# A fourth modulation vector of layer 1 computed on VectorE, and its pieces spread over the first FFN

## The chip, the cores and the metric

The kernel runs on one core of a Trainium2 chip. The metric is the device time of one execution in microseconds (us); three timed runs of the kernel before gave 1013.0 to 1016.56, with a median of 1015.02. The trace comes from one further execution of 1012.26 us. Its span, from the first to the last instruction in the trace, is 1010.5 us; the 1.8 us between them lie around the program.

The engines are named as in the trace: PE is TensorE's matmul, DVE is VectorE, ACT is ScalarE, POOL is GpSimd, SP is SyncE, whose queue issues nearly all weight transfers.

## What is computed

A two-layer trunk works on 384 tokens of width 1024: 256 latent tokens, which use the condition vector `c`, and 128 context tokens, which use `c_ctx`. Layer 0 is latent attention, layer 1 differential attention; each is followed by a convolutional FFN. Every sub-layer is modulated by vectors that come from the two condition vectors through one large matrix per layer (adaLN):

```python
cond_ctx = jax.nn.silu(c_ctx)[None, :]
cond_lat = jax.nn.silu(c)
for i in range(DEPTH):
    mod_p = jnp.split((cond_ctx @ ada_w[i] + ada_b[i])[:, None, :], N_MOD, axis=-1)   # N_MOD = 6
    mod_s = jnp.split((cond_lat @ ada_w[i] + ada_b[i])[:, None, :], N_MOD, axis=-1)
    hp = _modulate(yp, norm1_g[i], mod_p[0], mod_p[1])      # _rms(x, g) * (1 + scale) + shift
    ...                                                     # mixer; yp = yp + mod_p[2] * mp
    yp = yp + mod_p[5] * _conv_ffn(_modulate(yp, norm2_g[i], mod_p[3], mod_p[4]), *fprm)
    ...                                                     # the same for ys with mod_s

def _conv_ffn(h, w_in, conv_w, conv_b, w_out):
    a = _dwconv3(h @ w_in, conv_w) + conv_b
    g, up = jnp.split(a, 2, axis=-1)
    return (jax.nn.silu(g) * up) @ w_out
```

So each of the six vectors of a layer is a product of two condition vectors with a 1024x1024 block of `ada_w`. The change is about vector 4 of layer 1, the scale of that layer's FFN. It is first used in the norm ahead of that FFN, behind the whole attention of layer 1.

## The kernel before

**Weights.** Weights come from HBM in pieces of at most 128x1024 fp32 (512 KB) into a ring of seven buffers (`raw`, RAW_BUFS = 7), in the order of the plan below, by one queue on SP. A piece waits in that queue until the piece seven places earlier has been read for the last time. Weights of the big products are split into two fp32r parts, `whi` (a cast on ACT, L237) and `wlo` (a subtraction on DVE, L238), in rings of five pieces each (SPLIT_BUFS = 5), and each product is three matmuls (L320 to L322). Pieces marked WHOLE are read as they are.

**The first FFN.** Its hidden part has 22 steps `ffn0.in`; each takes two weight pieces (halves of the contraction) and gives two 128x384 results in PSUM, `fg` and `fu`, by 48 matmuls (L320 to L322). Behind it come the convolution (ACT L612, then eight DVE operations L614 and L616), SiLU, the product `hx` and its split `xh`, `xl`. Then eight steps `ffn0.out` follow, in the order 1, 2, 5, 3, 6, 0, 4, 7, each with three pieces of `w_out` (1024, 896 and 896 columns), 66 matmuls into `fo`, and the addition to `yT` (DVE L535). After the last, the norm of layer 1 leads to `diff.begin` and its projections `dkq0` (result `pd`).

**Modulation vectors.** They are made in two ways. `ada_block` runs on PE: eight weight pieces (rows of the contraction) are each multiplied by both conditions in four small matmuls on 32 columns of the array (L400); they gather in the PSUM tile `ada` (tag "a", one buffer), which DVE copies out (L414), and two transposes (`adat`, L421) bring it into place. `gemv_block` runs on DVE: eight rows of the transposed matrix are each multiplied by the condition, broadcast over all partitions in `condb`, and summed along the row by the same operation (L442). Each row takes two such operations, one for each condition: the first writes its products into `junk`, the second into the row's own buffer, which it frees. Such an operation is called a column here. Vectors 0, 1 and 3 of layer 1 (`vec0`, `vec1`, `vec3`) are made so, vector 4 (`vec4`) by `ada_block`; the gate of the attention (`gate1a`) also goes through `ada_block` and takes the PSUM tile `ada` behind `vec4`.

**Order.** The string SCHEDULE lists all steps; instructions and weight pieces are emitted in its order, and when the program is built a scheduler with its own estimates may still move instructions within an engine. The order of each engine is then fixed; an instruction that waits holds all behind it on that engine.

Of the kernel before, what the change touches and what calls it, by code (L numbers as in the profile page):

```python
# [186 lines left out]
vec3.5 ffn0.out2 vec3.1 vec3.4 ffn0.out5 ffn0.out3 ffn0.out6 ffn0.out0 vec4.5 vec4.4 gate1a.0 vec4.1 vec3.7 vec3.3
vec3.t vec4.6 vec4.7 ffn0.out4 ffn0.out7 vec4.t gate1a.2 diff.begin dkq0.claim gate1a.3 gate1a.6 dkq0 gate1a.5
gate1a.1 gate1a.4 gate1a.7 dv0.00 gate1a.t dv0.01 dv0.10 dv0.11 dk0.t0 dq0.t1 dv0.20 dq0.t0 diff0.s0 dk1.00 dv0.21
dk1.01 diff0.s1 dk0.t1 dk1.10 dk1.11 dk1.20 dq1.00 dq1.01 diff0.s2 dk1.21 diff1.s0 dq1.10 dq1.11 dq1.20 diff0.t0  # L190
diff1.s1 dq1.21 dk1.t0 dk1.t1 diff0.t2 dv1.00 dv1.01 dk2.00 dk2.01 dv1.10 diff0.t1 dv1.20 dv1.21 dq1.t0 dv1.11
diff1.s2 dq1.t1 diff2.s0 diff0.v dk2.10 diff1.t0 diff1.t2 diff1.t1 dk2.11 dk2.20 diff2.s1 diff2.s2 dk2.21 dq2.00
dq2.01 dq2.10 dq2.11 dk2.t0 diff1.v diff2.t1 dq2.20 diff0.ot dv2.00 diff2.t0 diff3.s0 dq2.t0 diff2.t2 dq2.21 dk2.t1
diff3.s1 diff3.s2 dv2.01 dq2.t1 dv2.10 dv2.11 dv2.20 diff2.v diff4.s0 dk3.00 diff3.t1 dk3.01 diff3.t0 dv2.21 diff1.ot
diff3.t2 diff4.s1 diff4.s2 dk3.10 dk3.20 dk3.21 dk3.11 dq3.00 diff3.v diff2.ot dq3.01 dk3.t0 diff5.s0 dq3.10 dv3.00
dq3.11 diff5.s1 diff4.t1 dk3.t1 dq3.20 diff4.t2 dq3.21 dv3.01 dv3.10 diff5.s2 diff3.ot dq3.t0 diff4.t0 dv3.11 dq3.t1
dv3.20 dv3.21 diff6.s0 wo1.low0 diff4.v diff5.t1 diff6.s1 diff5.t0 diff6.s2 diff5.t2 diff7.s0 diff6.t1 diff5.v
diff4.ot diff7.s1 wo1.low1 diff6.t0 wo1.low4 diff7.s2 wo1.low2 diff6.t2 wo1.low3 diff5.ot wo1.low5 wo1.low6 wo1.part0
diff7.t0 diff6.v diff7.t2 diff7.t1 wo1.low7 diff6.ot diff7.v wo1.part1 diff7.ot diff.end wo1.full2 wo1.full0 wo1.full1
wo1.full3 wo1.full6 ffn1.begin wo1.full4 wo1.full5 wo1.full7 ffn1.norm ffn1.claim gate1f.0 gate1f.1 gate1f.2 gate1f.3  # L200
gate1f.4 gate1f.6 gate1f.5 gate1f.7 gate1f.t ffn1.in01 ffn1.in2 ffn1.in3 ffn1.in4 ffn1.in5 ffn1.in6 ffn1.in7 ffn1.in8
# [1261 lines left out]
```

## Time and profile before

| what | value |
|---|---|
| median of three timed runs | 1015.02 us (1013.0 to 1016.56) |
| profiled execution, its span | 1012.26 us, 1010.5 us |
| PE busy | 984.3 us, 97% of the span |
| DVE busy | 740.4 us, 73% |
| ACT busy | 522.0 us, 52% |
| transfers | 160.54 MB, mean 159 GB/s |
| granted TensorE clock | 0.999 of full speed |

The shares are means over stages that differ much, so each stage is read by itself. The first FFN lies between about 237 and 525 us of the span: its hidden steps to 427 us, its output steps from 428 to 525 us.

### The profile page before, as it was taken

What the parts mean: (1) busy time and instruction counts of PE and PEld (TensorE: products, weight loads), DVE (VectorE), ACT (ScalarE), POOL (GpSimd) and SP (SyncE); (2) the same over time, 40 slices, a digit from 0 to 9 for tenths busy, and PEclk for the clock granted to TensorE, in tenths of its full rate; (3) what the DMA queues carried; (4) which work ended last, traced back from release to release, by engine and by line L of the source; (5) the groups of instructions that cost most, each with busy time, mean ns of one, the idle gap of its engine ahead of it and who ended that gap; (6) DMA issues with size and microseconds to landing.
All of it is one profiled execution on the core that took longest, in us unless ns stands there. A gap on an engine that the chain in (4) does not pass through costs nothing.

```text
span 1010.5 us, 16897 instructions
## 1 busy us (share of the span) xinstructions
PE 984.3 (97%) x6280; PEld 919.0 (91%) x6280; DVE 740.4 (73%) x1860; ACT 522.0 (52%) x1104; POOL 20.6 (2%) x48
## 2 busy tenths in 40 slices
...
GB/s 345 277 281 220 172 93 96 204 68 305 113 171 190 188 180 197 211 234 142 195 213 246 103 100 95 100 90 63 174 203 126 125 126 126 120 115 139 136 57 19
DMA packets 46226, 160.54 MB, mean 159 GB/s; under 512 B 5472, under 2 KB 6752, under 8 KB 46016
## 3 DMA queue, kind: packets, MB, share of 16 engines
...
q8 instruction: 49, 0.80, 0.3%
...
## 4 chain that ended last, share of the span: by engine, by line
PE 87%; DVE 5%; DMA 4%; ACT 2%; issue 1%; POOL 0%; DVEq 0%; ACTq 0%
PE fg L322 6%; PE fg L321 6%; PE fg L320 6%; PE fu L322 6%; PE fu L320 6%; PE fu L321 6%; PE fo L321 5%; PE fo L320 5%; PE fo L322 5%; PE pd L320 3%; PE pd L321 3%; PE pd L322 3%; PE wo L320 2%; PE wo L322 2%; PE wo L321 2%; PE ada L400 2%
## 5 line engine op out<-in xcount | busy, mean ns | idle before, releaser
L237 ACT CAST whi<-raw 128x512 fp32r<-128x512 f32 (+3 forms) x273 | 213.2, 801 | 221.9 <-PE fo L321 91.8
L238 DVE TENSOR_TENSOR wlo<-raw,whi 128x512 fp32r<-128x512 f32 (+3 forms) x273 | 245.0, 909 | 84.9 <-ACT whi L237 77.5
L322 PE MATMUL fg<-hh,wlo 128*128 128x384 f32 x352 | 117.9, 335 | 3.7 <-DVE wlo L238 3.7
L320 PE MATMUL fg<-hh,whi 128*128 128x384 f32 x352 | 118.2, 336 | 0.7 <-ACT hh L527 0.7
L321 PE MATMUL fg<-hl,whi 128*128 128x384 f32 x352 | 118.1, 335 | 0.0
L320 PE MATMUL fo<-xh,whi 128*128 128x384 f32 x352 | 117.8, 335 | 0.0
L320 PE MATMUL fu<-hh,whi 128*128 128x384 f32 x352 | 117.8, 335 | 0.0
L321 PE MATMUL fo<-xl,whi 128*128 128x384 f32 x352 | 117.7, 334 | 0.0
L322 PE MATMUL fu<-hh,wlo 128*128 128x384 f32 x352 | 117.6, 334 | 0.0
L321 PE MATMUL fu<-hl,whi 128*128 128x384 f32 x352 | 117.6, 334 | 0.0
L322 PE MATMUL fo<-xh,wlo 128*128 128x384 f32 x352 | 117.6, 334 | 0.0
L320 PE MATMUL pd<-whi,hh 128*128 128x256 f32 x288 | 83.9, 293 | 0.0
L321 PE MATMUL pd<-wlo,hh 128*128 128x256 f32 x288 | 82.3, 287 | 0.0
L322 PE MATMUL pd<-whi,hl 128*128 128x256 f32 x288 | 81.1, 284 | 0.0
L322 PEld LDWEIGHTS fg<-hh,wlo 128*128 128x128 f32 x352 | 66.1, 188 | 4.4 <-DVE wlo L238 4.3
L320 PEld LDWEIGHTS fg<-hh,whi 128*128 128x128 f32 x352 | 66.1, 188 | 2.0 <-ACT hh L527 1.5
L612 ACT ACTIVATE cva<-fg,small 128x384 f32<-128x384 f32 x44 | 29.7, 675 | 73.8 <-PE fg L322 73.8
L321 PEld LDWEIGHTS fg<-hl,whi 128*128 128x128 f32 x352 | 66.1, 188 | 1.2 <-DVE hl L528 0.8
L320 PEld LDWEIGHTS fo<-xh,whi 128*128 128x128 f32 x352 | 66.1, 188 | 0.8 <-ACT cva L612 0.4
L321 PEld LDWEIGHTS fo<-xl,whi 128*128 128x128 f32 x352 | 66.1, 188 | 0.4 <-issue 0.4
L320 PEld LDWEIGHTS fu<-hh,whi 128*128 128x128 f32 x352 | 66.1, 188 | 0.3
L322 PEld LDWEIGHTS fu<-hh,wlo 128*128 128x128 f32 x352 | 66.1, 188 | 0.0
(323 smaller groups left out, 2075.2 us busy)
## 6 DMA issues: line engine op xcount, KB each, us to landing
...
raw<-in_w_out SPq DMA_DIRECT2D x32, 448.0 KB, 3.4
...
```

The costliest lines, as they stand in the source:

```text
L237: self.nc.scalar.copy(hi[:, c], t[:, c])
L238: self.nc.vector.tensor_tensor(lo[:, c], t[:, c], hi[:, c].bitcast(F32), op=ALU.subtract)
L320: T.matmul(out, wh, xh, start=first, stop=False)
L321: T.matmul(out, wh, xl, start=False, stop=False)
L322: last_mm[0] = T.matmul(out, wl, xh, start=False, stop=last)
L400: T.matmul(st["acc"][32 * j:32 * j + 32, 0:w], conds[:, k, :], ws[c0 // 1024][:, c0 % 1024:c0 % 1024 + w], start=k == 0, stop=k == NK - 1, ...
L612: S.activation(a, acc, AF.Identity, bias=conv_b[:, l, j:j + 1], scale=w(1))
```

## The change

Vector 4 of layer 1 joins the vectors that DVE makes: its block of `ada_w` is handed over transposed with the others, and its `ada_block` goes. Each column becomes a step of its own, `a` for the first condition and `b` for the second, so that other steps can stand between the two; the row's buffer is held from `a` to `b`. All 64 columns are placed anew in SCHEDULE, beside the hidden steps from `ffn0.in3` on and beside the output steps.

```diff
-GEMV = ((1, 0), (1, 1), (1, 3))
+GEMV = ((1, 0), (1, 1), (1, 3), (1, 4))
...
-vec1.7 ffn0.in17 vec1.t ffn0.in18 vec3.0 ffn0.in19 ffn0.in20 vec4.0 vec3.2 ffn0.in21 vec4.2 vec4.3 ffn0.out1 vec3.6
+vec3.1a vec3.1b vec1.t ffn0.out5 vec3.2a vec3.2b vec3.3a vec3.3b vec3.4a vec3.4b ffn0.out3 vec3.5a vec3.5b vec3.6a
...
-        def row(i):
-            def fn(ws):
-                junk = phase["pool"].tile([P, D], mybir.dt.bfloat16, tag="junk", bufs=1, name=nm("junk"))
-                for c, out in enumerate((junk, ws[0])):
-                    V.scalar_tensor_tensor(out, ws[0], 1.0, phase["condb"][:, c, :], op0=ALU.mult, op1=ALU.mult,
-                                           accum_out=mod[l][:, 8 * v + i, c:c + 1])
-            step(f"{name}.{i}", fn, [(I["adat"][b, i], 1024, WHOLE)])
+        rows = {}
+
+        def row(i, c):
+            def fn(ws):
+                if c == 0:
+                    rows[i] = ws[0]
+                    out = phase["pool"].tile([P, D], mybir.dt.bfloat16, tag="junk", bufs=1, name=nm("junk"))
+                else:
+                    out = rows[i]
+                V.scalar_tensor_tensor(out, rows[i], 1.0, phase["condb"][:, c, :], op0=ALU.mult, op1=ALU.mult,
+                                       accum_out=mod[l][:, 8 * v + i, c:c + 1])
+            step(f"{name}.{i}{'ab'[c]}", fn, [(I["adat"][b, i], 1024, WHOLE)] if c == 0 else [])
...
         for i in range(NK):
-            row(i)
+            for c in range(2):
+                row(i, c)
...
     for b, (l, v) in enumerate(GEMV):
-        gemv_block(f"vec{v}", b, scale_of={1: 0}.get(v))
-    ada_block("vec4", 1, 4, 1, scale_of=1)
+        gemv_block(f"vec{v}", b, scale_of={1: 0, 4: 1}.get(v))
```

The lines of the changed file lie a little further down: L442 becomes L450, L238 L241, L535 L544, L400 L403, L320 to L322 become L323 to L325. Three places show what moves.

**DVE in the hidden steps**, behind the convolution of `ffn0.in8` in each kernel (`junk` and `raw` with `condb` are columns, `wlo` the second part of a weight piece, `cva` the next convolution). Before:

```order
L442 SCALAR_TENSOR_TENSOR junk_4002,mod_95<-raw_3906,condb 128x1024
L649 TENSOR_TENSOR hx_3983<-sg_3981,cva_3975 128x384
L442 SCALAR_TENSOR_TENSOR raw_3906,mod_95<-raw_3906,condb 128x1024
L546 TENSOR_TENSOR xl_3986<-hx_3983,xh_3985 128x384
L238 TENSOR_TENSOR wlo_4006<-raw_3917,whi_4005 128x1024
L238 TENSOR_TENSOR wlo_4082<-raw_3989,whi_4081 128x1024
L238 TENSOR_TENSOR wlo_4086<-raw_3991,whi_4085 128x1024
L442 SCALAR_TENSOR_TENSOR junk_4167,mod_95<-raw_4000,condb 128x1024
L238 TENSOR_TENSOR wlo_4176<-raw_4091,whi_4175 128x1024
L614 SCALAR_TENSOR_TENSOR cva_4061<-fg_4011,small,cva_4061 128x255
```

Now, at the same place:

```order
L241 TENSOR_TENSOR wlo_4153<-raw_3993,whi_4152 128x1024
L658 TENSOR_TENSOR hx_3973<-sg_3971,cva_3965 128x384
L241 TENSOR_TENSOR wlo_4157<-raw_4070,whi_4156 128x1024
L555 TENSOR_TENSOR xl_3976<-hx_3973,xh_3975 128x384
L450 SCALAR_TENSOR_TENSOR raw_3906,mod_95<-raw_3906,condb 128x1024
L450 SCALAR_TENSOR_TENSOR junk_4243,mod_95<-raw_4072,condb 128x1024
L623 SCALAR_TENSOR_TENSOR cva_4046<-fg_3996,small,cva_4046 128x255
```

Before, four weight pieces and three columns stand between two convolutions, with a column ahead of the first piece; now two pieces come first and two columns behind them.

**DVE in the output steps**, from the addition of one output step to that of the next (`fo_5257` in the kernel before and `fo_5215` in the changed one are the second output step). Before:

```order
L535 SCALAR_TENSOR_TENSOR yT<-fo_5257,mod_94,yT 128x256
L535 SCALAR_TENSOR_TENSOR yT<-fo_5257,mod_94,yT 128x128
L238 TENSOR_TENSOR wlo_5436<-raw_5343,whi_5435 128x896
L498 TENSOR_TENSOR sqa_5328<-sq_5227,sq_5326 128x384
L238 TENSOR_TENSOR wlo_5446<-raw_5352,whi_5445 128x896
L238 TENSOR_TENSOR wlo_5523<-raw_5439,whi_5522 128x1024
L535 SCALAR_TENSOR_TENSOR yT<-fo_5358,mod_94,yT 128x256
L535 SCALAR_TENSOR_TENSOR yT<-fo_5358,mod_94,yT 128x128
```

Now, up to the next addition:

```order
L544 SCALAR_TENSOR_TENSOR yT<-fo_5215,mod_94,yT 128x256
L544 SCALAR_TENSOR_TENSOR yT<-fo_5215,mod_94,yT 128x128
L241 TENSOR_TENSOR wlo_5415<-raw_5394,whi_5414 128x896
L507 TENSOR_TENSOR sqa_5286<-sq_5181,sq_5284 128x384
L450 SCALAR_TENSOR_TENSOR junk_5504,mod_95<-raw_5400,condb 128x1024
L450 SCALAR_TENSOR_TENSOR raw_5400,mod_95<-raw_5400,condb 128x1024
L241 TENSOR_TENSOR wlo_5422<-raw_5396,whi_5421 128x896
L450 SCALAR_TENSOR_TENSOR junk_5509,mod_95<-raw_5409,condb 128x1024
L450 SCALAR_TENSOR_TENSOR raw_5409,mod_95<-raw_5409,condb 128x1024
L241 TENSOR_TENSOR wlo_5512<-raw_5498,whi_5511 128x1024
L450 SCALAR_TENSOR_TENSOR junk_5518,mod_95<-raw_5418,condb 128x1024
L450 SCALAR_TENSOR_TENSOR raw_5418,mod_95<-raw_5418,condb 128x1024
```

Six columns, of three rows, stand between the three weight pieces where there was none.

**PE between two output steps**, the sixth and the seventh (`ada_5040` is vector 4's PSUM tile, `ada_5723` and `ada_5732` the gate's). Before:

```order
L322 MATMUL fo_5632<-xh_5126,wlo_5628 128x384
L400 MATMUL ada_5040<-raw_5621,conds 32x256 x4
L400 MATMUL ada_5040<-raw_5623,conds 32x256 x4
L400 MATMUL ada_5040<-raw_5705,conds 32x256 x4
L400 MATMUL ada_5040<-raw_5715,conds 32x256 x4
L400 MATMUL ada_5040<-raw_5721,conds 32x256 x4
L320 MATMUL fo_5773<-xh_3373,whi_5751 128x384
L321 MATMUL fo_5773<-xl_3374,whi_5751 128x384
L322 MATMUL fo_5773<-xh_3373,wlo_5752 128x384
L320 MATMUL fo_5773<-xh_3393,whi_5751 128x384
L400 MATMUL ada_5723<-raw_5625,conds 32x256 x4
```

Now:

```order
L324 MATMUL fo_5638<-xl_5088,whi_5633 128x384
L325 MATMUL fo_5638<-xh_5087,wlo_5634 128x384
L403 MATMUL ada_5732<-raw_5630,conds 32x256 x4
L323 MATMUL fo_5747<-xh_3373,whi_5725 128x384
L324 MATMUL fo_5747<-xl_3374,whi_5725 128x384
L325 MATMUL fo_5747<-xh_3373,wlo_5726 128x384
```

The five pieces of vector 4 are gone there, and the gate's first piece has moved from behind the fourth matmul of the seventh output step to ahead of its first.

## Rows read from the trace of the kernel before

**Rows 1.** The page's busy time, share of the span and instructions by engine.
```profile
PE 984.3 (97%) x6280; PEld 919.0 (91%) x6280; DVE 740.4 (73%) x1860; ACT 522.0 (52%) x1104; POOL 20.6 (2%) x48
```

**Rows 2.** Who PE waited for, 237 to 530 us: total us, times, longest.
```profile
PE fg L322 <- DVE wlo L238: 3.7, 2, 1.9
PE ada L400 <- DVE adas L414: 1.5, 1, 1.5
```

**Rows 3.** Busy us (instructions) of PE, PEld, DVE, ACT, POOL; clock, DMA share, GB/s.
```profile
313.00:341.00 28.00, 24.34 (x138) 23.62 (x138) 26.50 (x53) 11.81 (x17) 0.00 (x0) 1.00 0.56 180
341.00:428.00 87.00, 87.00 (x516) 85.47 (x515) 83.79 (x165) 44.48 (x64) 0.00 (x0) 1.00 0.62 200
...
451.30:462.80 11.50, 11.50 (x68) 11.50 (x67) 4.68 (x7) 3.50 (x5) 0.00 (x0) 1.00 0.41 126
...
474.20:485.60 11.40, 11.40 (x68) 11.40 (x67) 8.30 (x14) 2.23 (x3) 0.00 (x0) 1.00 0.66 216
```

**Rows 4.** DVE in order of time: start, us, line, operation, [idle before <-releaser]; stall.
```profile
318.28 1.22 DVE L442 SCALAR_TENSOR_TENSOR raw<-raw,condb 128x1024 f32<-128x1024 f32 x1
...
319.90 3.49 DVE L238 TENSOR_TENSOR wlo<-raw,whi 128x1024 fp32r<-128x1024 f32 x3
```

**Rows 5.** PE in order of time, the same stall.
```profile
321.17 0.45 PE L322 MATMUL fg<-hh,wlo 128*128 128x384 f32 x1 [1.77 <-DVE wlo L238]
```

**Rows 6.** PE in order of time: all pieces of vector 4, and the gate's first.
```profile
417.98 0.64 PE L400 MATMUL ada<-raw,conds 128*32 128x256 f32 x8
...
427.10 1.07 PE L400 MATMUL ada<-raw,conds 128*32 128x256 f32 x16
...
496.95 2.37 PE L400 MATMUL ada<-raw,conds 128*32 128x256 f32 x40
...
501.76 0.64 PE L400 MATMUL ada<-raw,conds 128*32 128x256 f32 x8 [1.53 <-DVE adas L414]
```

**Rows 7.** DVE in order of time: three convolutions, three additions, the copy.
```profile
409.95 0.74 DVE L614 SCALAR_TENSOR_TENSOR cva<-fg,small,cva 128x255 f32<-128x255 f32 x2 [0.15 <-ACT cva L612]
...
418.27 0.74 DVE L614 SCALAR_TENSOR_TENSOR cva<-fg,small,cva 128x255 f32<-128x255 f32 x2 [1.29 <-ACT cva L612]
...
427.39 0.74 DVE L614 SCALAR_TENSOR_TENSOR cva<-fg,small,cva 128x255 f32<-128x255 f32 x2
...
497.06 0.74 DVE L535 SCALAR_TENSOR_TENSOR yT<-fo,mod,yT 128x256 f32<-128x256 f32 x2 [1.88 <-PE fo L322]
499.81 1.09 DVE L238 TENSOR_TENSOR wlo<-raw,whi 128x896 fp32r<-128x896 f32 x1 [2.01 <-ACT whi L237]
...
501.29 0.42 DVE L414 COPY adas<-ada 128x256 f32<-128x256 f32 x1
...
513.41 0.74 DVE L535 SCALAR_TENSOR_TENSOR yT<-fo,mod,yT 128x256 f32<-128x256 f32 x2 [1.82 <-PE fo L322]
...
524.85 0.74 DVE L535 SCALAR_TENSOR_TENSOR yT<-fo,mod,yT 128x256 f32<-128x256 f32 x2 [1.82 <-PE fo L322]
```

**Rows 8.** PE and ACT in order of time, between the FFN and `dkq0`.
```profile
528.24 0.44 PE L421 MATMUL adat<-ident,adas 128*128 128x128 f32 x2
...
530.50 0.39 PE L320 MATMUL pd<-whi,hh 128*128 128x256 f32 x1
...
529.93 0.51 ACT L527 ACTIVATE hh<-mt,mod 128x256 fp32r<-128x256 f32 x1 [2.01 <-DVE mt L523]
```

**Rows 9.** DVE by form, 237 to 530 us: count, busy us, mean ns, idle before.
```profile
L238 DVE TENSOR_TENSOR wlo<-raw,whi 128x1024 fp32r<-128x1024 f32 x48 | 58.1, 1218 | 11.7 <-ACT whi L237 11.7
L442 DVE SCALAR_TENSOR_TENSOR junk<-raw,condb 128x1024 bf16<-128x1024 f32 x24 | 29.2, 1217 | 0.1
...
L238 DVE TENSOR_TENSOR wlo<-raw,whi 128x896 fp32r<-128x896 f32 x16 | 17.3, 1089 | 14.9 <-ACT whi L237 14.5
```

**Rows 10.** The page's DMA issues: count, KB each, median us to landing.
```profile
raw<-in_w_out SPq DMA_DIRECT2D x32, 448.0 KB, 3.4
```

**Rows 11.** ACT in order of time, weight casts near the end of the output steps.
```profile
487.14 1.05 ACT L237 CAST whi<-raw 128x1024 fp32r<-128x1024 f32 x1 [7.99 <-DMA raw<-in_w_out]
...
493.11 0.95 ACT L237 CAST whi<-raw 128x896 fp32r<-128x896 f32 x1 [4.49 <-DMA raw<-in_w_out]
```

More of the change, by code (lines that the diff above doesn't have):

```diff
@@ L182 @@
 wo0.full0 wo0.full3 wo0.full4 wo0.full6 wo0.part1 wo0.full5 wo0.full1 wo0.full7 gate0f.0 gate0f.6 ffn0.begin gate0f.5
-mod0f.t gate0f.3 ffn0.claim ffn0.norm gate0f.4 gate0f.1 gate0f.2 gate0f.7 ffn0.in01 ffn0.in2 vec0.0 gate0f.t ffn0.in3
-ffn0.in4 vec0.4 ffn0.in5 vec0.3 ffn0.in6 vec1.1 ffn0.in7 vec0.5 ffn0.in8 vec0.6 vec0.1 ffn0.in9 ffn0.in10 vec0.7
-vec1.6 vec1.0 ffn0.in11 vec0.2 ffn0.in12 vec1.2 vec0.t ffn0.in13 vec1.3 ffn0.in14 vec1.4 ffn0.in15 vec1.5 ffn0.in16
-vec1.7 ffn0.in17 vec1.t ffn0.in18 vec3.0 ffn0.in19 ffn0.in20 vec4.0 vec3.2 ffn0.in21 vec4.2 vec4.3 ffn0.out1 vec3.6
@@ L187 @@
[L187 to L201, printed above, removed]
@@ L202 @@
-ffn1.in9 ffn1.in10 ffn1.in11 ffn1.in12 ffn1.in13 ffn1.in14 ffn1.in15 ffn1.in16 ffn1.in17 ffn1.in18 ffn1.in19 ffn1.in20
-ffn1.in21 ffn1.out1 ffn1.out0 ffn1.out6 ffn1.out3 ffn1.out2 ffn1.out4 ffn1.out5 ffn1.out7
+mod0f.t gate0f.3 ffn0.claim ffn0.norm gate0f.4 gate0f.1 gate0f.2 gate0f.7 ffn0.in01 ffn0.in2 gate0f.t ffn0.in3 vec0.0a
+ffn0.in4 vec0.0b ffn0.in5 vec0.1a vec0.1b ffn0.in6 vec0.2a ffn0.in7 vec0.2b ffn0.in8 vec0.3a vec0.3b ffn0.in9 vec0.4a
+ffn0.in10 vec0.4b ffn0.in11 vec0.5a vec0.5b ffn0.in12 vec0.6a ffn0.in13 vec0.6b vec0.7a ffn0.in14 vec0.7b vec0.t
@@ new lines @@
+ffn0.in15 vec1.0a ffn0.in16 vec1.0b vec1.1a ffn0.in17 vec1.1b ffn0.in18 vec1.2a ffn0.in19 vec1.2b vec1.3a ffn0.in20
+vec1.3b ffn0.in21 vec1.4a vec1.4b ffn0.out1 vec1.5a vec1.5b vec1.6a vec1.6b vec1.7a ffn0.out2 vec1.7b vec3.0a vec3.0b
+vec3.1a vec3.1b vec1.t ffn0.out5 vec3.2a vec3.2b vec3.3a vec3.3b vec3.4a vec3.4b ffn0.out3 vec3.5a vec3.5b vec3.6a
+vec3.6b vec3.7a ffn0.out6 vec3.7b vec4.0a vec4.0b vec4.1a vec4.1b vec4.2a vec3.t ffn0.out0 vec4.2b vec4.3a vec4.3b
+vec4.4a vec4.4b gate1a.0 ffn0.out4 vec4.5a vec4.5b vec4.6a vec4.6b vec4.7a vec4.7b vec4.t ffn0.out7 gate1a.2
@@ new lines @@
+diff.begin dkq0.claim gate1a.3 gate1a.6 dkq0 gate1a.5 gate1a.1 gate1a.4 gate1a.7 dv0.00 gate1a.t dv0.01 dv0.10 dv0.11
+dk0.t0 dq0.t1 dv0.20 dq0.t0 diff0.s0 dk1.00 dv0.21 dk1.01 diff0.s1 dk0.t1 dk1.10 dk1.11 dk1.20 dq1.00 dq1.01 diff0.s2
+dk1.21 diff1.s0 dq1.10 dq1.11 dq1.20 diff0.t0 diff1.s1 dq1.21 dk1.t0 dk1.t1 diff0.t2 dv1.00 dv1.01 dk2.00 dk2.01
+dv1.10 diff0.t1 dv1.20 dv1.21 dq1.t0 dv1.11 diff1.s2 dq1.t1 diff2.s0 diff0.v dk2.10 diff1.t0 diff1.t2 diff1.t1 dk2.11
+dk2.20 diff2.s1 diff2.s2 dk2.21 dq2.00 dq2.01 dq2.10 dq2.11 dk2.t0 diff1.v diff2.t1 dq2.20 diff0.ot dv2.00 diff2.t0
```

11 lines of the change are left out of this document (added).

## The prediction

> **What bounds the kernel now.** I read the page's busy times first: PE is busy 97% of the span [rows 1], so what counts is what PE executes and where it stands still. In the first FFN, where the change lies, the list of waits shows two kinds of standstill [rows 2]: 3.7 us for `wlo` in the hidden steps, and 1.5 us for the copy of vector 4 in the output steps. The table by stages says where the first lies: between 313 and 341 us PE is busy 24.34 of 28.00 us, in the 87 us behind that without a gap [rows 3]. The order of time then says why. At 318.28 DVE runs a column, at 319.90 three `wlo` in a row [rows 4], and PE resumes at 321.17 after 1.77 us without work, just behind the first of them [rows 5]. DVE is no bound as a whole, but here it is 26.50 us busy of 28 [rows 3], and two columns (1.217 us each, [rows 9]) stood ahead of a piece that PE was about to need.
>
> The second kind: five pieces of vector 4 run on PE at 496.95, and the gate's first piece, which takes the same PSUM tile, has to wait until 501.76 [rows 6] for a copy that DVE starts at 501.29, because that copy stands in DVE's queue behind a `wlo` of 499.81 that had waited 2.01 us for ACT [rows 7]. ACT in turn waited for a transfer [rows 11].
>
> **The change part by part.** A hidden step lasts 418.27 - 409.95 = 8.32 us on PE, from convolution to convolution; an output step 524.85 - 513.41 = 11.44 us, from addition to addition [rows 7].
>
> 1. Vector 4's matmuls go: one, two and five pieces (8, 16 and 40 instructions, [rows 6]). The first: the convolutions around it are 427.39 - 418.27 = 9.12 us apart, so it costs 0.80 us [rows 7]. The second cannot be measured against a regular spacing; 16 instructions are busy 1.07 us [rows 6], twice the first would be 1.60, and I take 1.1. The third, with the gate's first piece and its wait: the step from 497.06 to 513.41 lasts 16.35 us, 4.91 more than its neighbour [rows 7]. Of this the gate's piece stays, at 0.80 like the other piece of 8, so 4.11 us go, the wait of 1.53 us among them [rows 6]. Nothing takes the wait's place: the gate's tile has no earlier owner any more, and its piece of weights can be loaded two output steps ahead. Sum of this part 0.80 + 1.1 + 4.11 = 6.0 us, all on PE, the engine that sets the end.
>
> 2. The waits of the hidden steps, 28.00 - 24.34 = 3.66 us [rows 3]. What late `wlo` depend on is how many columns stand ahead of them. Counted in the two orders, from the convolution of `ffn0.in2` to that of `ffn0.in12`: 22 columns before, 15 now; to the first addition to `yT` 42 and 35, and 6 and 29 in the output steps behind it. At each convolution I also counted the pieces already split beyond the step that it belongs to. Before, these are 5, 3, 2, 2, 2, 2, 1 from `ffn0.in2` to `ffn0.in8`, and in that place PE stalls; now 5, 4, 3, 3, 4, 4, 4, and 4 at each later step up to the sixth output step. Four pieces are two hidden steps, the one that PE is in and the whole next one, so a `wlo` may come 8 us late before PE sees it. A step with two pieces and two columns needs on DVE four operations of 1.22 us [rows 9] more than its convolution; 26.50 us busy in 28 [rows 3] is the same density, but with the lead it costs nothing. I take the whole 3.66; the bounds are 0 (the waits return elsewhere) and 3.66.
>
> 3. 29 columns beside the output steps. An output step used 4.68 us of DVE without columns and 8.30 with four and one piece of weights less than usual [rows 3]. With six columns and three pieces: 6 x 1.217 + 1.218 + 2 x 1.089 [rows 9] + 1.3 for addition and norm (4.68 less the three pieces) = 12.0 us against 11.44. Operations overlap a little at their ends, by up to 0.08 us each: three `wlo` of 1.218 take 3.49 in a row [rows 4, 9]. So a full step asks for 11.1 to 12.0 us; three such steps follow one another, the one ahead of them has seven columns, and DVE falls at most 2 to 3 us behind. Then a step with four columns and two with none let it catch up, before the norm needs it. What hides this is the lead of four pieces, an output step's three and one more; 11 us late is where PE would begin to wait. Cost 0; the bounds are 0 and 3 us (all of the lag lands on PE). Nothing is gained here.
>
> 4. Transfers: the same eight blocks of 512 KB, only from another array, and more of them beside the output steps: six pieces, 2.9 MB, in 11.44 us, 257 GB/s, where 216 was moved with a DMA share of 0.66 [rows 3]. A row holds its buffer from `a` to `b`, so a queue of seven buffers could run dry. From the release of a buffer to the `wlo` of the piece that takes it, 3.4 us of transfer [rows 10] and 1.05 of cast [rows 11] are needed. Counting DVE's work between these two places in the new order, the shortest stretches are 5.4 and 5.8 us in the hidden steps and 5.7 in the output steps; all others have 7.8 or more. Cost 0.
>
> 5. Ahead of `dkq0` the two transposes go (0.44 us), but PE starts there at 530.50, when `hh` of 529.93 is done [rows 8], and its waiting time was filled with the gate's pieces; DVE loses two small operations of that chain. I take 0.1 us, of 0 to 0.44.
>
> Sum: 6.0 + 3.66 + 0.1 = 9.8 us. The profiled execution of 1012.26 us would become 1002.5; it lies 2.8 us under the median of 1015.02, from which the forecast is **1005.2 us**.
>
> One rule speaks against the columns. Here 1024 elements with two fp32 sources take 1217 ns, as long as the plain subtraction of the same size, 1218 [rows 9]. The Trainium skill, "Vector Engine (DVE) Microarchitecture Reference", section 7 (points that are easy to get wrong), says that this very form of instruction runs at half its rate when both sources are in SBUF and not bf16; with the 0.96 GHz that the Trainium skill, "VectorE: DVE Perf Modes", section Specifications, gives, a column would take over 2.1 us, an estimate. The 29 columns of the output steps would then need 27 us more, and less the lead of 11 and the 9.8 gained the time would be 1021 or above. The trace does not agree with the rule for this form, so it gets no chance.
>
> **The rivals.** *The waits of the hidden steps stay.* A full step on DVE leaves next to nothing free, and if ACT's casts come late for a transfer, DVE stands and the next convolution slips. For it: the stretches of 5.4 and 5.8 us above are hardly longer than 4.5. Against: the lead does not fall below 3 in the new order. Time 1015.0 - 6.1 = 1008.9.
>
> *DVE's lag in the output steps reaches PE.* If some 3 us of it land there, through the late additions or late `wlo`: 1005.2 + 3 = 1008.2, with the waits of the hidden steps as well 1012.
>
> *The matmuls go and nothing is gained*, since the same stretch finds another wait of equal length, for instance the gate's first piece, which now stands ahead of the first matmul of its output step, on its transfer. For it: its buffer is taken over late from a row. Against: two steps lie between. Time 1013 to 1016.
>
> *Slower: the ring of buffers runs dry in the output steps.* Rows hold three of seven buffers, and each piece of weights waits for one, then for its transfer, cast and subtraction, one after the other. The trace has this pattern where PE-held pieces of vector 4 filled the ring: casts at 487.14 and 493.11, each released by a transfer, 5.97 us apart [rows 11]. Three pieces in a step would take 17.9 us instead of 11.44, 6.5 more; over five steps, less the lead of 11 and the 9.8 gained, the end is 12 us later, 1027. It decides from the point where more than four buffers are held by rows at once; in the new order no seven consecutive pieces have more than four rows among them.
>
> **How the numbers follow.** The forecast gets 0.74, the first rival 0.11, the second 0.06, nothing gained 0.05, slower 0.04. The forecast's own range is 1003 to 1008: 0.3 for the transposes and 0.5 for the two pieces at 427.10 below, and up to 1.5 on either side for the spread of the runs. For 8 in 10 I reach over the first rival and most of the second: 1002 to 1011. About 0.3%, 3.0 us, is what a measurement of this kernel can tell from no change; the forecast and the first two rivals are beyond it except for the end at 1012, so faster 0.90, the same 0.06, slower 0.04.
>
> **What would show it.** Right: no L403 between 410 and 500 us, the output steps 11.44 us apart but for 12.2 at the gate's piece, no wait of PE for `wlo` or for the copy in this FFN, its end some 9.7 us earlier, and DVE over 90% busy in output steps two to five. Wrong: a wait of PE for `wlo` in the hidden steps (part 2), steps longer than 11.5 us with DVE as releaser (part 3) or with ACT waiting for transfers (part 4), or a gate's piece that waits for its transfer (part 1).

## The result, and the profile after

| | before | after |
|---|---|---|
| time, median (runs) | 1014.01 us (4, 1011.73 to 1016.56) | 1001.20 us (4, 1000.96 to 1001.35) |
| profiled execution, span | 1012.26, 1010.5 us | 1001.30, 999.5 us |
| first `fg` to last `yT` of the first FFN | 237.30 to 524.85 = 287.55 us | 237.93 to 515.01 = 277.08 us |

The ratio is 0.9873, with an interval of 0.9847 to 0.9898: faster by 12.8 us. The forecast was 1005.2 us in a range of 1002 to 1011; the time lies 0.8 us below that range. From profile to profile the gain is 10.96 us, where 9.8 was forecast; from median to median it is larger still, and the four runs of after spread over 0.4 us where those of before spread over 5. That difference is what most of the experiments are about. One of the twelve runs of the kernel before in the second series took 1613.32 us at a mean clock of 0.559; it is in the median of 1014.47 us below, and in no range or count.

The busy times on the page answer to [rows 1]:

```profile
PE 978.0 (98%) x6214; PEld 917.6 (92%) x6214; DVE 759.1 (76%) x1891; ACT 520.3 (52%) x1104; POOL 19.9 (2%) x48
```

PE has 66 instructions fewer (64 of vector 4 and two transposes) and is busy 6.3 us less; DVE is busy 18.7 us more. The list of what PE waited for from 237 to 520 us (total, times, longest), against [rows 2]:

```profile
PE fg L323 <- ACT hh L536: 0.7, 1, 0.7
```

Neither `wlo` nor the copy of vector 4 is in it; what is left, the wait ahead of the first `fg`, stood there before too with 0.7 us. The stages, with the columns of [rows 3]: the stretch that held the two waits, the rest of the hidden steps, and output steps three to five, each from one addition to `yT` to the next:

```profile
313.00:341.00 28.00, 28.00 (x163) 28.00 (x162) 25.84 (x52) 14.58 (x21) 0.00 (x0) 1.00 0.51 170
341.00:428.00 87.00, 87.00 (x504) 87.00 (x503) 82.32 (x164) 44.76 (x65) 0.00 (x0) 1.00 0.55 177
446.50:458.10 11.60, 11.60 (x69) 11.60 (x68) 11.50 (x21) 3.47 (x4) 0.00 (x0) 1.00 0.81 262
458.00:469.60 11.60, 11.60 (x69) 11.60 (x68) 11.53 (x22) 3.47 (x4) 0.00 (x0) 1.00 0.80 276
469.50:481.10 11.60, 11.60 (x69) 11.60 (x68) 11.49 (x21) 3.48 (x4) 0.00 (x0) 1.00 0.81 265
```

PE has no gap any more; in the output steps DVE has next to none either (11.5 of 11.6 us), and PE does not feel it. DVE in order of time, from the end of one output step to the end of the next, shows how it fits (start, us, line, operation):

```profile
458.06 0.74 DVE L544 SCALAR_TENSOR_TENSOR yT<-fo,mod,yT 128x256 f32<-128x256 f32 x2
458.71 1.08 DVE L241 TENSOR_TENSOR wlo<-raw,whi 128x896 fp32r<-128x896 f32 x1
459.71 0.55 DVE L507 TENSOR_TENSOR sqa<-sqa,sq 128x384 f32<-128x384 f32 x1
460.18 1.22 DVE L450 SCALAR_TENSOR_TENSOR junk<-raw,condb 128x1024 bf16<-128x1024 f32 x1
...
463.60 1.22 DVE L450 SCALAR_TENSOR_TENSOR junk<-raw,condb 128x1024 bf16<-128x1024 f32 x1
464.74 0.09 DVE L450 DVE_READ_ACCUMULATOR junk<-raw,condb 128x1 f32 x1
464.86 1.22 DVE L450 SCALAR_TENSOR_TENSOR raw<-raw,condb 128x1024 f32<-128x1024 f32 x1
...
469.56 0.74 DVE L544 SCALAR_TENSOR_TENSOR yT<-fo,mod,yT 128x256 f32<-128x256 f32 x2
```

The additions come 11.50 us apart, with no wait for PE in front of them: DVE, not PE, sets their time. Without any columns (an experiment below) the first of the two stands at 456.92, so DVE is 1.1 us late, the 0.07 us between the starts of the two FFNs taken off. Two output steps later it has caught up and waits for PE again; the last two steps, against [rows 7]:

```profile
491.34 0.74 DVE L544 SCALAR_TENSOR_TENSOR yT<-fo,mod,yT 128x256 f32<-128x256 f32 x2 [0.79 <-PE fo L325]
503.57 0.74 DVE L544 SCALAR_TENSOR_TENSOR yT<-fo,mod,yT 128x256 f32<-128x256 f32 x2 [1.83 <-PE fo L325]
515.01 0.74 DVE L544 SCALAR_TENSOR_TENSOR yT<-fo,mod,yT 128x256 f32<-128x256 f32 x2 [1.82 <-PE fo L325]
```

PE holds the gate's first piece between these, now without a wait, and begins `dkq0` 9.9 us earlier, against [rows 6] and [rows 8]:

```profile
491.23 0.64 PE L403 MATMUL ada<-raw,conds 128*32 128x256 f32 x8
...
520.60 0.39 PE L323 MATMUL pd<-whi,hh 128*128 128x256 f32 x1 [0.42 <-ACT hh L536]
```

### The profile page after: what moved, and what is told of

It is laid out like the page before. It is cut to its first block, busy times and chain, and to the rows that moved or that the text cites. A ratio compares the mean times of both kernels' runs of the same rounds, so it can differ in the third digit from the quotient of the medians.

```text
span 999.5 us, 16802 instructions
## 1 busy us (share of the span) xinstructions
PE 978.0 (98%) x6214; PEld 917.6 (92%) x6214; DVE 759.1 (76%) x1891; ACT 520.3 (52%) x1104; POOL 19.9 (2%) x48
## 4 chain that ended last, share of the span: by engine, by line
PE 93%; DVE 3%; DMA 2%; ACT 1%; issue 1%; POOL 0%; DVEq 0%; ACTq 0%
PE fg L324 6%; PE fg L323 6%; PE fu L323 6%; PE fo L323 6%; PE fo L325 6%; PE fu L325 6%; PE fg L325 6%; PE fu L324 6%; PE fo L324 6%; PE pd L323 3%; PE pd L324 3%; PE pd L325 3%; PE wo L323 2%; PE wo L324 2%; PE wo L325 2%; PE ada L403 1%
## 5 line engine op out<-in xcount | busy, mean ns | idle before, releaser
L241 DVE TENSOR_TENSOR wlo<-raw,whi 128x512 fp32r<-128x512 f32 (+3 forms) x273 | 245.6, 910 | 65.6 <-ACT whi L240 54.7
L323 PE MATMUL fg<-hh,whi 128*128 128x384 f32 x352 | 117.9, 335 | 0.7 <-ACT hh L536 0.7
L323 PE MATMUL fu<-hh,whi 128*128 128x384 f32 x352 | 117.8, 335 | 0.0
L323 PE MATMUL fo<-xh,whi 128*128 128x384 f32 x352 | 117.7, 334 | 0.0
L325 PE MATMUL fu<-hh,wlo 128*128 128x384 f32 x352 | 117.6, 334 | 0.0
L325 PE MATMUL fg<-hh,wlo 128*128 128x384 f32 x352 | 117.6, 334 | 0.0
L325 PE MATMUL fo<-xh,wlo 128*128 128x384 f32 x352 | 117.6, 334 | 0.0
L323 PE MATMUL pd<-whi,hh 128*128 128x256 f32 x288 | 83.9, 292 | 0.4 <-ACT hh L536 0.4
L325 PE MATMUL pd<-whi,hl 128*128 128x256 f32 x288 | 81.4, 284 | 0.0
L323 PEld LDWEIGHTS fg<-hh,whi 128*128 128x128 f32 x352 | 66.0, 188 | 1.2 <-ACT hh L536 1.2
L323 PEld LDWEIGHTS fo<-xh,whi 128*128 128x128 f32 x352 | 66.1, 188 | 0.4 <-issue 0.4
L323 PEld LDWEIGHTS fu<-hh,whi 128*128 128x128 f32 x352 | 66.1, 188 | 0.3
L325 PEld LDWEIGHTS fu<-hh,wlo 128*128 128x128 f32 x352 | 66.1, 188 | 0.0
L325 PEld LDWEIGHTS fo<-xh,wlo 128*128 128x128 f32 x352 | 66.1, 188 | 0.0
```

Source lines behind the costliest of these rows:

```text
L241: self.nc.vector.tensor_tensor(lo[:, c], t[:, c], hi[:, c].bitcast(F32), op=ALU.subtract)
L323: T.matmul(out, wh, xh, start=first, stop=False)
L325: last_mm[0] = T.matmul(out, wl, xh, start=False, stop=last)
```

## The experiments

Each ratio is to runs of the kernel before that were taken beside the experiment. The measure used for all of them is the length of the first FFN in the profiled execution, from the start of its first `fg` to its last addition to `yT`, since the start-up ahead of it differs by up to 1.6 us from kernel to kernel:

| kernel | first `fg` | last `yT` | between | median of the runs (lowest to highest) |
|---|---|---|---|---|
| before, profile shown | 237.30 | 524.85 | 287.55 | see above |
| before again | 238.49 | 527.34 | 288.85 | 1014.47 (1012.10 to 1017.65) |
| vector 4 on PE, columns placed as after | 237.85 | 519.39 | 281.54 | 1006.56 (1005.75 to 1008.06) |
| vector 4 on DVE, columns placed as before | 238.62 | 523.49 | 284.87 | 1009.43 (1007.27 to 1010.82) |
| after without columns | 237.86 | 514.92 | 277.06 | 1001.75 (1001.38 to 1002.89) |
| after, second profile | 238.50 | 515.56 | 277.06 | 1000.81 (999.80 to 1001.98) |
| after, columns of a row joined | 237.48 | 514.54 | 277.06 | 1000.98 (999.92 to 1001.23) |
| after, gate's piece late | 238.22 | 514.48 | 276.26 | 1002.61 (1002.29 to 1003.19) |
| after with two standstills | 237.69 | 520.79 | 283.10 | 1011.48 (1008.62 to 1013.55) |
| after with one standstill | 237.58 | 519.14 | 281.56 | 1004.96 (1004.42 to 1006.47) |
| after with the memsets alone | 237.24 | 515.05 | 277.81 | 1002.52 (1001.45 to 1003.85) |
| before, 22 columns spread | 237.01 | 526.48 | 289.47 | 1015.01 (1012.75 to 1016.52) |
| before, 18 columns spread | 238.13 | 522.33 | 284.20 | 1010.09 (1008.47 to 1011.19) |

**The kernel before, once more.** No edit.

> The kernel before once more, with its own profile, to see what its runs differ in: they lie between 1011.7 and 1016.6 us, those of the changed kernel between 1001.0 and 1001.4. Theory S (the spread comes from the waits that the change removes): the spans of two profiles differ in the first FFN alone, between the first convolution and the last addition to yT, by as much as their times differ, and the waits for wlo of 313 to 341 us or the long step at 497 to 513 us have another length; all other stages agree within 0.5 us. Rival S2 (the spread has nothing to do with the change, for example in the start-up or in the second attention): the difference lies outside the first FFN. Time 1011.5 to 1016.5 either way.

Measured: 1014.47 us, ratio to before 0.9992 (0.9975 to 1.0009). The waits for `wlo` have their old length, 3.6 us; the wait for the copy is 1.1 us instead of 1.5. What differs is PE's granted clock (the column after POOL's), in five stretches of this profile:

```profile
322.40:341.70 19.30, 17.45 (x98) 16.84 (x98) 18.49 (x37) 9.49 (x13) 0.00 (x0) 1.00 0.56 191
341.80:342.80 1.00, 1.00 (x6) 1.00 (x7) 1.00 (x2) 0.00 (x0) 0.00 (x0) 1.00 0.87 344
342.80:346.20 3.40, 3.40 (x13) 3.40 (x12) 3.40 (x5) 1.05 (x1) 0.00 (x0) 0.50 0.90 304
346.40:350.00 3.60, 3.60 (x22) 3.60 (x21) 2.74 (x9) 2.70 (x4) 0.00 (x0) 1.00 0.81 281
...
80.00:83.40 3.40, 3.40 (x9) 1.30 (x8) 2.17 (x9) 0.36 (x2) 0.54 (x1) 0.50 0.56 207
```

PE resumes at 341.71 after its second wait for `wlo` (1.86 us); 1.1 us later it runs at 1.2 GHz for 3.4 us, 13 matmuls, against 22 in the 3.6 us behind that at 2.4 GHz. That costs 1.7 us, and 287.55 + 1.7 - 0.4 (the shorter wait for the copy) gives the 288.85 measured. The profile that the prediction was made from has the same waits for `wlo` and a clock of 1.00 in both places, and everywhere else while PE works. The mean of 0.999 that its run has comes from the end, where PE has nothing left to do:

```profile
1005.00:1008.00 3.00, 1.07 (x7) 0.75 (x5) 0.74 (x2) 0.00 (x0) 0.00 (x0) 1.00 0.09 32
...
1009.60:1010.00 0.40, 0.00 (x0) 0.00 (x0) 0.00 (x0) 0.00 (x0) 0.00 (x0) 0.50 0.00 0
```

So a mean of 0.999 is no sign of a fall during the work. One fall of 3.4 us takes 1.7 of 1010 us, an estimate of 0.0017 of the mean: runs at 0.998 or less hold one or more. Since one of the two falls lies at 80 us, ahead of the FFN, theory S holds in part: waits go ahead of both, but the change removes only those of the FFN. Over the 62 runs of the kernel before that the experiments brought along, the time goes with the mean clock of the run (correlation -0.84): median 1012.1 us at 1.000 (5 runs), 1014.1 at 0.998 (21), 1016.2 at 0.996 (15), 1.04 us for each 0.001. Of the 62, 50 are at 0.998 or less. At a clock that does not fall the kernel before takes about 1012 us (the five runs at 1.000: 1011.99 to 1014.69), not 1014.5.

**The places alone.** Vector 4 back on PE, the rest as after:

```diff
-GEMV = ((1, 0), (1, 1), (1, 3), (1, 4))
+GEMV = ((1, 0), (1, 1), (1, 3))
...
-... vec3.t ffn0.out0 vec4.2b vec4.3a vec4.3b vec4.4a vec4.4b gate1a.0 ffn0.out4 ...
+... vec3.t ffn0.out0 vec4.5 vec4.4 gate1a.0 vec4.1 vec4.6 vec4.7 ffn0.out4 ...
...
+    ada_block("vec4", 1, 4, 1, scale_of=1)
```

> The columns of vectors 0, 1 and 3 are split and placed as in the changed kernel; vector 4 stays on PE at its places of before. Theory T (the two gains are separate): the waits of the hidden steps go, 3.7 us, and the matmuls of vector 4 with the wait for the copy stay, so 1012.26 - 3.7 = 1008.6 us for a profile like that of before, and 1009 to 1010.5 for the median. If the spread of before comes from the hidden waits, its runs lie within 0.5 us. Rival R1 (the waits went because vector 4 left, not because of the places): within 1 us of before.

Measured: 1006.56 us, ratio 0.9920 (0.9905 to 0.9935), faster than theory T gave, and with a spread of 2.3 us where 0.5 was expected. PE's waits in the FFN are down to one, and the wait for the copy went as well, since DVE had no late `wlo` in front of it:

```profile
PE fg L322 <- ACT hh L535: 0.7, 1, 0.7
```

The 281.54 us stand 4.48 above the floor of 277.06, which is what vector 4's 64 matmuls cost; and 6.01 below before, which is what all the waits cost (the clock is 1.00 throughout the FFN in all three profiles). Rival R1 falls.

**The move alone.** Vector 4 on DVE beside the output steps, whole rows, the hidden steps as before:

```diff
-GEMV = ((1, 0), (1, 1), (1, 3))
+GEMV = ((1, 0), (1, 1), (1, 3), (1, 4))
...
-... ffn0.in18 vec3.0 ffn0.in19 ffn0.in20 vec4.0 vec3.2 ffn0.in21 vec4.2 vec4.3 ffn0.out1 ...
+... ffn0.in18 vec3.0 ffn0.in19 ffn0.in20 vec3.2 ffn0.in21 ffn0.out1 ...
-... ffn0.out5 ffn0.out3 ffn0.out6 ffn0.out0 vec4.5 vec4.4 gate1a.0 vec4.1 ...
+... ffn0.out5 vec3.7 vec3.3 vec3.t ffn0.out3 vec4.0 vec4.1 ffn0.out6 vec4.2 vec4.3 ffn0.out0 vec4.4 vec4.5 gate1a.0 ...
```

> Vector 4 goes to VectorE in whole rows beside the output steps; the rows of vectors 0, 1 and 3 in the hidden steps stay whole and where they were before (two of vector 3 that stood in a later output step stand two steps earlier). Theory T: 6.0 us for the matmuls and the wait go, the waits of the hidden steps stay at 3 to 4 us, so 1006.3 us for a profile like that of before, 1006 to 1008.5 for the median, and the spread of before stays if it comes from the hidden waits. Rival R1: the hidden waits go as well, about 1002 us.

Measured: 1009.43 us, ratio 0.9943 (0.9926 to 0.9961), slightly above theory T's upper end, with a spread of 3.6 us. PE's waits, and the clock behind them:

```profile
PE fg L322 <- DVE wlo L238: 3.6, 2, 1.8
PE fg L320 <- ACT whi L237: 1.7, 1, 1.7
...
345.00:348.20 3.20, 3.20 (x12) 3.20 (x11) 3.09 (x5) 1.05 (x1) 0.00 (x0) 0.50 0.84 284
```

The waits for `wlo` stay when vector 4 is gone, so its matmuls were not their cause; one for a cast came on top, and the clock fell again.

**No columns.** Columns and their rows' transfers left out, so that the biases stand in place of the four vectors:

```diff
-            step(f"{name}.{i}{'ab'[c]}", fn, [(I["adat"][b, i], 1024, WHOLE)] if c == 0 else [])
+            step(f"{name}.{i}{'ab'[c]}", lambda ws: None)
...
-            V.tensor_tensor(mod[l][:, cs, :], mod[l][:, cs, :], ada_b[:, l, cs, :], op=ALU.add)
+            V.tensor_copy(mod[l][:, cs, :], ada_b[:, l, cs, :])
```

> The changed kernel without any of the 64 columns and without the transfers of their rows: the four vectors are left out (the biases stand in their place). Theory T (columns and transfers are hidden beside PE): as the changed kernel within 1 us, 1000.2 to 1001.5. Rival R3 (the columns still cost PE some time, by late pieces, late additions or shared memory): 998 us or less.

Measured: 1001.75 us (0.25 above the upper end), 277.06 us for the FFN. With all 64 columns after takes 277.08. They cost nothing: theory T, and R3 falls.

**The kernel after, once more.** No edit.

> The changed kernel once more, for the spread of its runs. In the second profile of before the granted clock is 0.50 for 3.4 us behind the second wait for wlo (342.8 to 346.2 us) and again for 3.4 us behind the two waits for cqh and cql (80.0 to 83.4 us), at 1.00 in the profile that the prediction was made from. Theory C (the forecast missed because before's median holds such falls of the clock, which follow the waits that the change removes): the changed kernel keeps only the waits at 78 to 80 us; most runs at 1001.0 to 1001.5 us with a mean clock of 1.000, a few 1 to 2 us above at 0.998 or 0.999. Rival S2 (the spread is another thing): a spread of 3 to 5 us like that of before.

Measured: 1000.81 us, ratio 0.9868 (0.9853 to 0.9882), 999.8 to 1002.0, every run at a clock of 1.000. Theory C, though the runs spread 2.2 us without any fall, more than I had expected. The waits at 78 to 80 us were followed by a fall in one profile of before and in neither of after. The kernels of the table whose FFN has no wait for `wlo`, a cast, the copy, a memset or a transfer (after twice, its variants without columns, joined and with the memsets alone, and the places alone) have 26 runs, 3 of them at 0.998 and none lower, against the 50 of 62 of before. The falls are nearly gone with the standstills, not wholly; where those three lie no profile shows.

**Two standstills put back.** The decisive one for the clock:

```diff
...
+                if l == 0 and j in (10, 12):
+                    g, d = phase["gap"], ps("a", "gap")
+                    T.matmul(d[0:32, 0:2], conds[:, 0, :], g[:, 0:2], start=True, stop=True)
+                    for _ in range(4):
+                        G.memset(g, 0.0)
+                    stall = T.matmul(d[0:32, 0:2], conds[:, 0, :], g[:, 0:2], start=True, stop=True)
...
-                half([acc], ws[0:1], 0)
+                with behind(stall):
+                    half([acc], ws[0:1], 0)
```

> The changed kernel with two standstills of PE put back by themselves: in the tenth and twelfth hidden step a matmul of 2 columns, four memsets of 128x512 on GpSimd, which wait for it, and another such matmul, behind which the step begins. From the memsets of before (128x256 in 311 ns, 128x128 in 223 ns) each standstill should be 2.0 to 2.4 us, about 17 us apart, as the two of before were 1.8 and 1.9 us, 19 us apart; no column and no piece of weights moves. Theory C: the time rises by the standstills, 4.0 to 4.8 us, and in part of the runs by 1.7 us more, with the clock at 0.50 for 3.4 us behind one of them: runs between 1005.2 and 1009, mean clock 0.998 or less in those above 1006.5. Rival S2 (the clock falls for another reason, such as the load on DVE or the transfers): all runs within 0.5 us, at 1005.2 to 1006, clock 1.000.

Measured: 1011.48 us, 12 runs from 1008.6 to 1013.6. PE's waits, and one standstill in order of time:

```profile
PE gap L694 <- POOL gap L693: 4.8, 2, 2.4
PE pd L323 <- ACT hh L536: 1.5, 2, 1.1
...
325.12 0.22 PE L694 MATMUL gap<-gap,conds 128*32 128x2 f32 x2 [2.38 <-POOL gap L693]
```

This profile is of the fastest run, at clock 1.000: the FFN is 6.04 us longer for 4.8 us of waiting, and the boundary waits 1.1 us more. Two of the 12 runs have the full clock (1008.6 and 1009.4), the others 0.999 to 0.994, and the two at 0.994 take 1013.5 us. So the changed kernel, which spread over 0.4 to 2.2 us, spreads over 5 again as soon as PE stands still twice. Theory C, with both sizes too small: a standstill costs 3.0 us where 2.0 to 2.4 were expected, and 9 of the 12 runs are at 0.998 or less.

**One standstill.** Against the kernel with two:

```diff
-                if l == 0 and j in (10, 12):
+                if l == 0 and j in (10,):
```

> As gap2 with the first of its two standstills alone, in the tenth hidden step. In the profile of gap2 a standstill takes 2.4 us of waiting and about 3.0 us in all, and the wait for hh ahead of pd grew by up to 1.1 us beside them. Theory C1 (each standstill by itself can be followed by a fall of the clock): fastest runs at 1004 to 1005 us with a clock of 1.000, a part of the runs 1.7 us above at 0.998. Rival C2 (it takes two, some 17 us apart): all runs at 0.999 or above, within 0.7 us.

Measured: 1004.96 us, ratio 0.9909 (0.9894 to 0.9925). Four of the six runs take 1004.4 to 1005.2 us at a clock of 0.999 or 1.000, the other two 1006.3 and 1006.5 at 0.998 and 0.999. The profile is of a run at 0.998; three stretches of it, the standstill, then the work behind it:

```profile
322.60:325.00 2.40, 0.03 (x1) 0.03 (x2) 2.40 (x8) 1.92 (x4) 2.10 (x4) 1.00 0.72 247
325.40:328.60 3.20, 3.20 (x11) 3.20 (x12) 3.20 (x7) 0.51 (x1) 0.00 (x0) 0.52 0.23 45
...
328.80:332.00 3.20, 3.20 (x21) 3.20 (x20) 1.35 (x3) 1.04 (x1) 0.00 (x0) 1.00 0.85 271
```

One standstill of 2.4 us is followed at once by half clock until 328.5 us; 281.56 is 4.48 above the changed kernel, 2.8 for the standstill and 1.7 for the clock. C1 holds, C2 falls.

**The memsets without the standstill.** Against the kernel with two standstills:

```diff
-                    stall = T.matmul(d[0:32, 0:2], conds[:, 0, :], g[:, 0:2], start=True, stop=True)
```

> As gap2, but PE does not wait for the memsets: the second matmul of each standstill is left out. Theory C (PE's standing still is what the clock follows): as the changed kernel, 1001.0 to 1001.8 us, clock 1.000. Rival (GpSimd's memsets, through the memory that they share with VectorE, or the small matmuls are what costs): 1003 us or more.

Measured: 1002.52 us, four runs from 1001.5 to 1003.9, ratio 0.9883 (0.9863 to 0.9902), against 0.9868 (0.9853 to 0.9882) for after. The clock of the profiled run is 1.00 throughout the FFN; one run of the four, that of 1003.9, is at 0.998. The median lies between the two expectations. In its profile the FFN is 0.75 us longer than the floor of 277.06, so that most of the remaining 1 us seems to belong to the memsets and small matmuls that are left; it is not the 7 to 12 us by which the runs with two standstills lie above the changed kernel.

**Joined columns.**

```diff
                 if c == 0:
                     rows[i] = ws[0]
-                    out = phase["pool"].tile([P, D], mybir.dt.bfloat16, tag="junk", bufs=1, name=nm("junk"))
+                    return
```

(the second step of a row then runs both columns)

> The changed kernel with the two columns of a row run together, at the place of the second. Theory T (the number of columns ahead of each piece of weights decides, not the split): 1001.2 us within 0.7, no wait for wlo above 0.3 us. Rival R2 (the split into single columns is what removed the waits, since two in a row hold a wlo up by 2.4 us): waits for wlo of 1 us or more come back, 1002.5 to 1005 us.

Measured: 1000.98 us, 277.06 us, no wait for `wlo`. The split is not needed; R2 falls.

**22 columns, spread.** In the kernel before:

```diff
-... ffn0.in3 ffn0.in4 ... ffn0.in8 vec0.6 vec0.1 ffn0.in9 ffn0.in10 vec0.7 vec1.6 vec1.0 ffn0.in11 ...
+... ffn0.in3 vec1.0 ffn0.in4 ... ffn0.in8 vec0.6 ffn0.in9 vec0.1 ffn0.in10 vec0.7 vec1.6 ffn0.in11 ...
```

> The kernel before with two rows moved: vec0.1 from the eighth to the ninth hidden step, vec1.0 from the tenth to the third, so that no step has more than four columns behind it where two had four and six. From in2 to in12 there are still 22 columns, and vector 4 stays on PE. The prediction's count (the number of columns ahead of a piece of weights decides): the waits for wlo stay at 3 to 4 us, median 1013 to 1015 us. Rival R4 (the clusters of four and six columns between two convolutions decide): the waits fall to 1 us or less, the falls of the clock behind them go too, median 1009 to 1011 us.

Measured: 1015.01 us, ratio 1.0004 (0.9990 to 1.0017), no change. PE's waits:

```profile
PE fu L320 <- DVE cva L616: 1.9, 1, 1.9
PE fg L322 <- DVE wlo L238: 1.5, 1, 1.5
```

The standstill is 3.4 us, nearly the 3.7 of before, but more than half of it now has another name: the convolution that frees a PSUM tile comes late instead of a `wlo`. One place still has four columns between two convolutions, but DVE runs them from 336 us on, behind the standstill (PE resumes at 333.46 and 335.79 us); ahead of it there are at most three. The prediction's count holds, R4 falls.

**18 columns, spread.**

```diff
-... ffn0.in8 vec0.6 vec0.1 ffn0.in9 ffn0.in10 vec0.7 vec1.6 vec1.0 ffn0.in11 ...
+... ffn0.in8 vec0.6 ffn0.in9 vec0.1 ffn0.in10 vec0.7 ffn0.in11 ...
-... vec1.7 ffn0.in17 vec1.t ffn0.in18 vec3.0 ffn0.in19 ffn0.in20 ...
+... vec1.7 ffn0.in17 vec1.6 ffn0.in18 vec3.0 ffn0.in19 vec1.0 vec1.t ffn0.in20 ...
```

> The kernel before with three rows moved: vec0.1 from the eighth to the ninth hidden step, vec1.6 and vec1.0 from the tenth to the seventeenth and nineteenth, so 18 columns from in2 to in12 and no step with more than two behind it in that stretch. By the count and by the clusters alike the waits for wlo go, 3.7 us, and the falls of the clock with them: median 1007 to 1010 us, near place_only. If the waits stay above 1 us, neither is the cause, and the lead of the split pieces is what remains.

Measured: 1010.09 us, ratio 0.9955 (0.9938 to 0.9971). PE's waits:

```profile
PE ada L400 <- DVE adas L414: 1.4, 1, 1.4
...
PE fg L322 <- DVE wlo L238: 0.4, 1, 0.4
...
404.78 0.44 PE L322 MATMUL fg<-hh,wlo 128*128 128x384 f32 x1 [0.45 <-DVE wlo L238]
```

Four columns fewer take the wait for `wlo` out of that stretch altogether; the 0.4 us that is left lies at 404.78 us, behind the steps that the two rows were moved to. With the 22 of the kernel above, this speaks for part 2: DVE has too much to do there in sum. How evenly it comes matters less; since this kernel has fewer columns and no step with more than two at once, the two are not wholly parted.

**The gate's piece late**, a try for a faster version:

```diff
-... vec4.4a vec4.4b gate1a.0 ffn0.out4 ... vec4.t ffn0.out7 gate1a.2 diff.begin ...
+... vec4.4a vec4.4b ffn0.out4 ... vec4.t ffn0.out7 gate1a.0 gate1a.2 diff.begin ...
```

> The changed kernel with the first piece of the gate vector moved from ahead of the seventh output step to behind the last, where PE waits for the norm. Theory: the step at 491 us lasts 11.44 instead of 12.23 us, 0.79 less; of this the gap ahead of the first pd, 0.42 us, takes some back, so 1000.4 to 1000.9 us. Rival (PE has no free time there, 3.2 us of such pieces already stand behind the norm's matmuls): 1001.2 us, no change.

Measured: 1002.61 us, slower than after by 1.4 to 1.8 us. The FFN is 0.80 us shorter, as expected, but the last piece ahead of `pd` now waits:

```profile
520.88 0.62 PE L403 MATMUL ada<-raw,conds 128*32 128x256 f32 x2 [1.23 <-DMA raw<-in_ada]
```

The piece that was moved keeps its buffer through two more output steps, and the last of the gate's pieces is loaded too late for its place: the last six of these pieces are asked for from 497.72 to 517.43 us, in the changed kernel from 493.30 to 513.55. From the last `yT` to `pd` PE loses 1.4 us by it, 0.6 net of the 0.80 gained; the rest of the 1.4 to 1.8 us lies outside and is not explained. So the changed kernel is the fastest here that computes everything, with the joined one equal to it.

## Why the prediction was wrong, step by step

**Part 1, vector 4's matmuls and the copy: right.** Without the wait of 1.53 us the 6.0 were 4.47 us; the run with the places alone shows 4.48.

**Part 2, the hidden waits: right in cause, too small in size.** The number of columns decides, as far as the two spread kernels can tell. (From `in2` to `in12` the trace has 23 before where 22 were counted, and 15 now as counted.) The waits of both kinds cost 6.01 us, where 3.66 + 1.53 = 5.19 were shown as idle. Nearly all of the remaining 0.8 us lies in the hidden steps. From the first `fg` to the first `fo` PE takes 428.10 - 237.30 = 190.80 us before and 424.26 - 237.85 = 186.41 with the places alone, 4.39 less, so the upper bound of 3.66 was no bound. Before, and with the places alone:

```profile
428.10 0.44 PE L320 MATMUL fo<-xh,whi 128*128 128x384 f32 x1
...
424.26 0.44 PE L322 MATMUL fo<-xh,whi 128*128 128x384 f32 x1
```

The matmuls around the first wait of before show how an idle figure falls short of the cost (the wait itself is [rows 5]):

```profile
318.89 0.33 PE L320 MATMUL fu<-hh,whi 128*128 128x384 f32 x1
319.06 0.34 PE L321 MATMUL fu<-hl,whi 128*128 128x384 f32 x1
...
321.45 0.34 PE L322 MATMUL fu<-hh,wlo 128*128 128x384 f32 x1
```

Matmuls of this size follow one another 0.17 us apart, each recorded with 0.33. The one behind the wait starts 2.11 us after the last, 1.94 too late, and the next 0.28 us behind it, 0.11 more: 2.05 us lost for 1.77 listed. The second wait loses 2.17 for 1.89.

**Part 3, 29 columns beside the output steps: right.** DVE 11.5 of 11.6 us busy, 1 us late instead of 2 to 3, and no cost to PE. The additions themselves do come more than 11.5 us apart, the first two 12.43 with seven columns between them, but the lead hides it from PE:

```profile
434.13 0.74 DVE L544 SCALAR_TENSOR_TENSOR yT<-fo,mod,yT 128x256 f32<-128x256 f32 x2
...
446.56 0.74 DVE L544 SCALAR_TENSOR_TENSOR yT<-fo,mod,yT 128x256 f32<-128x256 f32 x2
```

The rule of half rate that the prediction set against them is not seen in the 64 columns either (DVE by form; the mean of one in ns stands behind the busy time):

```profile
L450 DVE SCALAR_TENSOR_TENSOR raw<-raw,condb 128x1024 f32<-128x1024 f32 x32 | 39.1, 1223 | 0.6
L450 DVE SCALAR_TENSOR_TENSOR junk<-raw,condb 128x1024 bf16<-128x1024 f32 x32 | 39.0, 1220 | 0.1
```

**Part 4, transfers, and part 5, the boundary: right within 0.3 us.** No wait for a transfer in the FFN, at 262 to 276 GB/s (six pieces are 3.01 MB with 1024 bytes to the KB, 264 GB/s where the prediction has 257). From the last `yT` to `pd` PE takes 5.59 us instead of 5.65; the wait of 0.42 us ahead of `pd` replaces the transposes.

**From the profile to the median: this step failed.** It read "it lies 2.8 us under the median of 1015.02, from which the forecast is 1005.2": the distance of one execution from the median was carried over unchanged, and the spread of the runs was put at 1.5 us on either side. That distance is for the most part no property of the measurement but a term of the kernel: a standstill of PE is in part of the executions followed by 3.4 us at half clock, 1.7 us each time. The profiled execution had met none; that it was such a one was luck, and so was about 0.5 of the 2.8 us, since the median of 62 runs is 1014.53. With the standstills gone nearly all falls go too, and after has its profile at 1001.30 and its median at 1001.20 us; two standstills put back bring falls and spread back, their memsets alone do not. The miss of 4.0 us is then 2.8 for this step and 1.2 between the profiles: 0.8 in the FFN (part 2), the rest the balance of a start-up that is 0.6 us longer and later stages that are some 1.1 us shorter, which no run explains. With 1002.5, the sum from the profile without the offset, the forecast would have been 1.3 us off, and the range moved down by the same 2.8 us would have held the result.

The rows before could not show a fall of the clock, but they had its trace: three runs 3.6 us apart, and a profiled execution faster than all three. The rivals did not hold the possibility that waits cost more than their length.

**The rivals.** None came: no wait stayed, DVE's lag did not reach PE, the gate's piece did not wait for its transfer, the ring of buffers did not run dry.
